# Joining the running maximum and the row sums of an attention sweep with VectorE instead of TensorE transposes

## The chip, the cores and the metric

The kernel runs on one core of a Trainium2 chip. The core has five engines that each take their instructions in a fixed order and wait for each other through semaphores: TensorE (PE, matrix products and transposes; its weight loads are listed apart as PEld), VectorE (DVE), ScalarE (ACT), GpSimd (POOL) and SyncE (SP, which here only issues DMAs). SBUF is the on-chip memory of 128 partitions, PSUM the memory that PE writes. Only PE, DVE and ACT touch PSUM.

The metric is the time of one execution on the device in microseconds (us); the median of the runs counts.

## The reference

One encoder layer over 2048 tokens of width 1024. One input projection feeds two mixers, a gated linear attention (group A) and a dense softmax attention with compressed keys and values (group B). Their outputs go side by side through one output projection, and a LayerNorm closes the layer. The change sits mainly in group B:

```python
def attend(blk):
    qn, qr = blk
    s = (jnp.einsum('bqhd,bkhd->bhqk', qn, k_nope) + jnp.einsum('bqhr,bkr->bhqk', qr, k_r))
    p = jax.nn.softmax(s, axis=-1)
    return jnp.einsum('bhqk,bkhv->bqhv', p.astype(v.dtype), v)
```

There are 4 heads and 2048 queries; the softmax runs over all 2048 keys. All arrays are float32.

## The kernel before

The program has four stages: sweep A (linear attention, first pass, to about 330 us), sweep C (second pass, and the projections that make queries and keys, to about 580 us), the attention, and the output projection with its LayerNorm, whose first part overlaps the end of the attention.

**The attention** works through 16 blocks, each one head times 512 queries (`QB`). Scores are kept transposed: keys on the 128 partitions, the 512 queries along the free axis. A block has 8 key pairs `j` of 2 x 128 keys. A float32 product is made of several fp32r products of high and low parts. Per block and pair:

- `scores` (L1599 to L1603): 10 matmuls into a PSUM tile `pS` of 128 x 2 x 512; two such tiles alternate.
- `copy` (ACT, L1608): the scores to an SBUF tile `s`.
- `smax` (DVE, L1618 and L1621): the running maximum over keys, `rm`, 128 x 512, from each half of `pS`.
- `sub` (DVE, L1645), `exp` (ACT, L1649), `phi` (ACT, high part `ph`, L364), `plo` (POOL, low part `pl`, L370), `pv` (6 matmuls into `o`, L418 to L420).
- `acc`: the sum of the exponentials, on DVE for pairs 0, 1, 2, 5 (PSUM tile `ap`, L1672), on POOL for pairs 3, 4, 6, 7 (SBUF tile `acc`, L1675 and L1677).

At the end of a block, the maximum must be joined over the 128 partitions and spread back: `tmax` (L1627) transposes `rm` on PE in 4 pieces into the PSUM tile `mx`; `rmax` (L1632) reduces it on DVE to `mc`, 128 x 4; `bmax` (L1639) transposes the broadcast `mc` on PE back into `mb`, one maximum per query on all partitions. `sub` needs `mb`. Likewise the sums: `tot` (L1695, L1696) adds the two partial sums into `acc`; `tsum` (L1708) transposes it on PE in 4 pieces into `sx`; `rcp` (L1714, L1715) reduces and inverts on DVE; `keep` (L1720) stores the 512 results to DRAM from ACT's queue.

**The order** is written out: every step has a place in units of one key pair (tables `PLACE`, `PLACE_LAST`), all steps are sorted by place, and each engine executes its instructions in just that order. While block `i` ends, PE already works on the scores of block `i+1` and on the `pv` products of block `i-1`. Sweep C is ordered in the same way by `PLACE_C`, `PLACE_C_FIRST` and `PLACE_C_LAST`.

**The close** (`finish`): per 128 tokens the LayerNorm, with `rsqrt_b` (L437 to L440) as four tiny DVE instructions on 128 x 1 columns, and scalings of 128 x 512 (L2023, L2026).

Of the kernel before, what the change touches and what calls it, by code (L numbers as in the profile page):

```python
# [9 lines left out]
F32 = mybir.dt.float32  # L10
# [3 lines left out]
ALU = mybir.AluOpType  # L14
AX = mybir.AxisListType
# [3 lines left out]
P = 128  # L19
# [10 lines left out]
QB = 512  # L30
# [43 lines left out]

SUM_DVE = (0, 1, 2, 5)
SUM_POOL = (3, 4, 6, 7)

# [65 lines left out]

PLACE_C = dict(
    skv=1.6,
    kvx=(1.12, 1.44),
    ipa=(-0.08, 0.695),
    ipb=(-0.014, 0.701),  # L150
    ipc=(0.026, 0.723),
# [3 lines left out]
    pqr=(0.849, 1.355),  # L155
    tq=(1.13, 1.56),
    xh=(-0.19, -0.054),
    sqO=(0.272, 0.988),
    rgl=(0.283, 1.029),
    sqm=(0.14, 0.858),  # L160
    rml=(0.352, 0.993),
# [13 lines left out]
    ssm=(0.277, 0.958),  # L175
    rmd=(0.401, 1.006),
# [47 lines left out]
    kvx=(1.18, 1.5),  # L224
# [9 lines left out]
    sqO=(0.469, 0.999),  # L234
    rgl=(0.603, 1.027),
    sqm=(0.073, 0.865),
    rml=(0.101, 0.976),
# [13 lines left out]
    ssm=(0.095, 0.913),  # L251
    rmd=(0.194, 1.009),
# [41 lines left out]
    sqO=(0.15, 0.435),  # L294
    rgl=(0.229, 0.457),
    sqm=(0.101, 0.657),
    rml=(0.162, 0.878),
    cq=(0.463, 1.041),
    ckv=(0.35, 1.075),
    vh=(0.865, 1.252),  # L300
# [7 lines left out]
    ss=(0.166, 0.454),  # L308
    rgd=(0.332, 0.461),
    og=(0.336, 0.508),  # L310
    ssm=(0.103, 0.733),
    rmd=(0.254, 1.022),
    krf=(0.139, 0.6),
    cqTl=(0.598, 1.211),
    ckvTl=(0.88, 1.703),
# [37 lines left out]
class K:  # L353
# [80 lines left out]

    def rsqrt_b(self, u, y, t, w, r):
        nc = self.nc
        nc.vector.tensor_tensor(t, y, u, ALU.mult)  # L437
        nc.vector.tensor_tensor(w, t, y, ALU.mult)
        nc.vector.tensor_scalar(t, w, -0.5, 1.5, ALU.mult, ALU.add)
        nc.vector.tensor_tensor(r, t, y, ALU.mult)  # L440
        return r
# [1133 lines left out]
    def attention(self):  # L1575
        tc, nc = self.tc, self.nc
        mm = nc.tensor.matmul
        V, G, Ac = nc.vector, nc.gpsimd, nc.scalar
        NP = NKT // 2
        with ExitStack() as ctx:  # L1580
# [29 lines left out]
            def smax(i, j):  # L1610

                d = stt[i]
                s = d["s"][j]
                ps = d["ps", j]
                src = s if i == 0 else ps
                if j == 0:
                    d["rm"] = self.keep.tile([P, QB], F32, tag="rm", name=f"rm{i}")
                    V.tensor_tensor(d["rm"], src[:, 0], s[:, 1], ALU.max)  # L1618
                else:
                    for e in range(2):  # L1620
                        V.tensor_tensor(d["rm"], src[:, e], d["rm"], ALU.max)  # L1621

            def tmax(i):
                d = stt[i]
                d["x"] = pX.tile([P, 4, P], F32, tag="x", name=f"mx{i}")
                for e in range(4):
                    nc.tensor.transpose(d["x"][:, e], d["rm"][:, e * P:(e + 1) * P], self.ident)  # L1627

            def rmax(i):
                d = stt[i]  # L1630
                d["mc"] = bs.tile([P, 4], F32, tag="mc", name=f"mc{i}")
                V.tensor_reduce(d["mc"], d["x"], AX.X, ALU.max)  # L1632

# [27 lines left out]
            def acc0(i):  # L1661
                d = stt[i]
                d["ap"] = pA.tile([P, QB], F32, tag="ap", name=f"ap{i}")
                Ac.activation(d["ap"], d["s"][SUM_DVE[0]][:, 0], AF.Copy)

            def acc(i, j):
                d = stt[i]
                s = d["s"][j]
                if j in SUM_DVE or i == nb - 1:
                    for e in range(2):  # L1670
                        if j != SUM_DVE[0] or e:
                            V.tensor_tensor(d["ap"], d["ap"], s[:, e], ALU.add)  # L1672
# [25 lines left out]
            def close(i, shape, name, other):  # L1698


                p, tag = other if i == nb - 1 else (pX, "x")
                return p.tile(shape, F32, tag=tag, name=name)

            def tsum(i):
                d = stt[i]
                d["x"] = close(i, [P, 4, P], f"sx{i}", (pA, "ap"))
                for e in range(4):
                    nc.tensor.transpose(d["x"][:, e], d["as"][:, 0, e * P:(e + 1) * P], self.ident)  # L1708

            def rcp(i):  # L1710

                d = stt[i]
                rc = bs.tile([P, 4], F32, tag="rc", name=f"rc{i}")
                V.tensor_reduce(rc, d["x"], AX.X, ALU.add)  # L1714
                V.reciprocal(rc, rc)  # L1715
                d["rc"] = rc

            def keep(i):
                h, b = blocks[i]
                Ac.dma_start(self.r_s[b][:, h].rearrange("o (e p) -> p (o e)", p=P), stt[i]["rc"])  # L1720

            def turn(i):

# [58 lines left out]
            own = (("tot", tot), ("tsum", tsum), ("rcp", rcp), ("keep", keep), ("oh", oh), ("ol", ol), ("y", y), ("yc", yc))  # L1782
            own_late = tuple(e for e in own if e[1] is not keep)
            for i in range(nb):
                for j in range(NP):
                    t = NP * i + j
                    put(t, scores, i, j)
                    for n, f in (("copy", copy), ("max", smax), ("sub", sub), ("exp", exp), ("hi", phi), ("lo", plo),
                                 ("pv", pv), ("acc", acc)):
                        if n != "acc" or j != SUM_POOL[0] or i == nb - 1:  # L1790
                            put(t + at(n, i, j), f, i, j)
                put(NP * i + at("acc0", i), acc0, i)
                for n, f in (("tmax", tmax), ("rmax", rmax), ("bmax", bmax)) + {nb - 1: (), nb - 2: own_late}.get(i, own):
                    put(NP * i + NP - 1 + at(n, i), f, i)
                if i + 2 < nb:
                    put(NP * i + 4.05, self.fetch, i + 2)

# [69 lines left out]
            for c in range(4, NCH):  # L1867
                with fixed():
                    split(c + 2)
                    load(c + 4)  # L1870
                    if 4 < c < NCH - 1:
                        op.load_res(rest[c + 1])
                    op.product(rest[c])
                    op.finish(rest[c])
                with self.after(*last.values()), fixed():
                    for f in {4: (tot, oh, ol), 5: (tsum, rcp), 7: (turn, y, rows, yc)}.get(c, ()):
                        f(nb - 1)
                    if c == 6:
                        turn(nb - 2)
                        rows(nb - 2)  # L1880
# [217 lines left out]
```

## Time and profile before

| | us |
|---|---|
| median of 3 runs (lowest, highest) | 1267.62 (1267.16, 1270.45) |
| the profiled execution | 1266.33 |
| its span, first to last instruction | 1264.5 |
| PE busy in the span | 1242.3 |
| DVE busy | 906.0 |
| ACT busy | 725.8 |
| POOL busy | 721.7 |

The span is 1.8 us shorter than the profiled execution's own time, and that execution is 1.3 us below the median. A timeline row of the profile reads: start (us), duration (us), engine, line, operation, output<-inputs, shape, xcount, and in brackets the idle time of the engine before it with what ended it. Rows that say x2 or more merge instructions that follow each other. A matmul's duration overlaps that of the next, so what a matmul costs is the distance from its start to the next start. On the other engines too the next instruction often starts some tens of ns before the row of the last has ended.

### The profile page before, as it was taken

Reading aid. Unit: us, or ns where it says so; the run is one execution under the profiler, and the core shown is the slowest. Engines: PE = TensorE matmul, PEld = TensorE weight load, DVE = VectorE, ACT = ScalarE, POOL = GpSimd, SP = SyncE. Lnnn points to the kernel's source line nnn. Section 1 sums busy time; section 2 is a strip of 40 time slices with the busy share of each in tenths; the row PEclk is TensorE's granted clock in tenths of the full one; section 3 lists DMA queues with packets and bytes.
Section 4 is the critical chain, followed back from the end, with each engine's and each line's share of the span. In section 5 each row is a group of like instructions: output and inputs, shape, how many; then the busy total and the mean of one; then the engine's idle time right before and its main releaser. Section 6 shows DMA issues by size and latency. Waiting matters only on the chain.

```text
span 1264.5 us, 19632 instructions
## 1 busy us (share of the span) xinstructions
PE 1242.3 (98%) x6890; PEld 1094.2 (87%) x6890; DVE 906.0 (72%) x1654; ACT 725.8 (57%) x1149; POOL 721.7 (57%) x443
## 2 busy tenths in 40 slices
PE   8999999999999999999999999999999999999997
PEld 7999999999899999988788888888888888887886
DVE  6635555554565666575988888888888888379998
ACT  7543443444664545445788888788888888411110
POOL 0132323223364555421798888889999999935441
PEclk9999999999999999999999999999999999999999
DMA  8224655556757788868422222202244120477773
GB/s 294 79 81 123 139 143 139 144 135 159 268 179 212 227 244 239 240 183 195 73 37 48 41 43 43 59 9 59 59 94 92 41 43 26 125 205 199 206 199 116
DMA packets 284338, 165.61 MB, mean 131 GB/s; under 512 B 185574, under 2 KB 241774, under 8 KB 284240
## 3 DMA queue, kind: packets, MB, share of 16 engines
q1 hardware_dynamic: 276176, 162.23, 48.2%
q0 software_dynamic: 672, 2.10, 0.4%
q8 instruction: 55, 0.90, 0.4%
q10 hardware_dynamic: 7392, 0.03, 0.3%
q14 instruction: 43, 0.35, 0.1%
HBM read 105.54 MB, written 58.75 MB: 130 GB/s over the span
## 4 chain that ended last, share of the span: by engine, by line
PE 86%; DVE 5%; DMA 3%; issue 2%; SPq 2%; ACT 1%; POOL 1%; DVEq 0%; POOLq 0%; ACTq 0%
PE pz L1266 7%; PE ipm L1335 5%; PE o L418 5%; PE o L419 5%; PE o L420 5%; PE pS L1599 4%; PE pS L1600 4%; PE pS L1602 4%; PE pS L1601 4%; PE pS L1603 4%; PE ipa L418 4%; PE ipa L420 4%; PE ipa L419 4%; PE ipg L420 2%; PE ipg L418 2%; PE ipg L419 2%
## 5 line engine op out<-in xcount | busy, mean ns | idle before, releaser
L370 POOL TENSOR_TENSOR pl<-s,ph 128x1024 fp32r<-128x1024 f32 x128 | 306.6, 2412 | 51.5 <-ACT ph L364 40.9
L1621 DVE TENSOR_TENSOR rm<-pS,rm 128x512 f32<-128x512 f32 x210 | 144.8, 690 | 36.3 <-ACT s L1608 30.7
L1608 ACT ACTIVATE s<-pS 128x1024 f32<-128x1024 f32 x128 | 131.3, 1025 | 60.4 <-PE pS L1603 50.0
L1645 DVE TENSOR_TENSOR s<-s,mb 128x1024 f32<-128x1024 f32 x128 | 151.2, 1213 | 8.9 <-PE mb L1639 8.8
L364 ACT ACTIVATE ph<-s 128x1024 fp32r<-128x1024 f32 x128 | 135.0, 1057 | 16.7 <-PE o L420 16.1
L1649 ACT ACTIVATE s<-s 128x1024 f32<-128x1024 f32 x128 | 131.4, 1049 | 9.4 <-DVE s L1645 9.3
L418 PE MATMUL ipa<-wah,xah 128*128 128x384 f32 (+1 forms) x384 | 128.8, 335 | 5.4 <-ACT wah L364 5.4
L419 PE MATMUL ipa<-wal,xah 128*128 128x384 f32 (+1 forms) x384 | 124.6, 324 | 0.0
L420 PE MATMUL ipa<-wah,xal 128*128 128x384 f32 (+1 forms) x384 | 124.4, 324 | 0.0
L1085 POOL TENSOR_TENSOR Sb<-Sb,Us 64x512 f32<-64x512 f32 x15 | 19.9, 1325 | 170.1 <-DVE Us L1077 161.0
L1599 PE MATMUL pS<-qh,kvT 128*128 128x512 f32 x256 | 102.4, 400 | 0.8 <-DVE rm L1621 0.4
L418 PE MATMUL o<-ph,vh 128*128 128x512 f32 x256 | 101.0, 395 | 0.0
L1600 PE MATMUL pS<-ql,kvT 128*128 128x512 f32 x256 | 99.9, 390 | 0.0
L1602 PE MATMUL pS<-rh,kvT 128*128 128x512 f32 x256 | 99.9, 390 | 0.0
L1601 PE MATMUL pS<-qh,kvT 128*128 128x512 f32 x256 | 99.8, 390 | 0.0
L1603 PE MATMUL pS<-rl,kvT 128*128 128x512 f32 x256 | 99.7, 390 | 0.0
L420 PE MATMUL o<-ph,vl 128*128 128x512 f32 x256 | 99.7, 389 | 0.0
L419 PE MATMUL o<-pl,vh 128*128 128x512 f32 x256 | 99.6, 389 | 0.0
L1672 DVE TENSOR_TENSOR ap<-ap,s 128x512 f32<-128x512 f32 x120 | 83.1, 693 | 2.7 <-ACT s L1649 0.8
L370 POOL TENSOR_TENSOR ol<-of,oh 128x512 fp32r<-128x512 f32 x32 | 43.7, 1365 | 67.8 <-ACT oh L364 62.5
L418 PEld LDWEIGHTS ipa<-wah,xah 128*128 128x128 f32 x384 | 73.1, 190 | 8.3 <-ACT wah L364 5.4
L419 PEld LDWEIGHTS ipa<-wal,xah 128*128 128x128 f32 x384 | 73.1, 190 | 1.0 <-DVE wal L370 0.5
(303 smaller groups left out, 3416.1 us busy)
## 6 DMA issues: line engine op xcount, KB each, us to landing
xcf<-xT_dram SPq DMA_DIRECT2D x16, 512.0 KB, 5.7
xr<-x_dram SPq DMA_DIRECT2D x16, 512.0 KB, 5.9
out_dram<-rr SPq DMA_DIRECT2D x32, 256.0 KB, 2.1
xaf<-xT_dram SPq DMA_DIRECT2D x14, 512.0 KB, 4.1
oib<-oi_s SPq DMA_DIRECT2D x16, 256.0 KB, 4.9
qdb<-qd_s SPq DMA_DIRECT2D x16, 256.0 KB, 3.7
SU<-su_s SPq DMA_DIRECT2D x16, 256.0 KB, 4.8
ub<-u_s SPq DMA_DIRECT2D x16, 256.0 KB, 4.5
```

The source lines that it names most:

```text
L364: return nc.scalar.activation(dst, src, AF.Copy).ins
L370: return e.tensor_tensor(dst, src, hi.bitcast(F32), ALU.subtract).ins
L418: mm(out, ah, bh, start=start, stop=False)
L419: mm(out, ah, bl, start=False, stop=False)
L420: mm(out, al, bh, start=False, stop=stop)
L1599: mm(ps[:, e], kh, qh, start=True, stop=False)
L1600: mm(ps[:, e], kh, ql, start=False, stop=False)
L1601: mm(ps[:, e], kl, qh, start=False, stop=False)
L1602: mm(ps[:, e], kr, rh, start=False, stop=False)
L1603: mm(ps[:, e], kr, rl, start=False, stop=True)
L1621: V.tensor_tensor(d["rm"], src[:, e], d["rm"], ALU.max)
L1645: V.tensor_tensor(s, s, d["mb"][:, None, :].to_broadcast([P, 2, QB]), ALU.subtract)
```

## The change

The edit has four parts.

1. **Maximum (blocks 1 to 10, `WIDE`).** `rm` becomes 128 x 2 x 512 in SBUF, a tile of the pool `xfp`. Pair 0 does nothing; pair 1 takes the maximum of its PSUM tile and pair 0's SBUF copy; pairs 2 to 7 take one 128 x 1024 instruction each instead of two of 128 x 512. The join no longer uses PE transposes: DVE takes the maximum of the two halves, transposes within 32 x 32 blocks, reduces to 128 x 16, folds the four 32-partition quadrants by two copies and one maximum, and writes the result to `mc` by four 32 x 4 instructions. `bmax` stays, at place 1.9 instead of 1.48.
2. **Sums (blocks 0 to 13).** A new step `tpart` does the same kind of transposing and reducing on DVE, to 128 x 16; `tsum` is then one PE transpose instead of four, `rcp` works on 16 x 32, and `keep` stores 16 rows of 32 values.
3. **`rsqrt_b` for one column** takes three `tensor_scalar` instructions with per-partition scalars instead of three `tensor_tensor` and one `tensor_scalar`. Only `finish` has one column.
4. **Places** in sweep C: `kvx` of each step's first chunk, `sqO` of each step's second, and `rml`, `ssm` of the last step.

```diff
+WIDE = range(1, 11)
-    tsum=12.04,
+    tpart=11.25,
+    tsum=12.44,
...
-    kvx=(1.12, 1.44),
+    kvx=(1.3, 1.44),
...
     def rsqrt_b(self, u, y, t, w, r):
         nc = self.nc
+        if u.shape[1] == 1:
+            nc.vector.tensor_scalar(t, y, u, y, ALU.mult, ALU.mult)
+            nc.vector.tensor_scalar(t, t, -0.5, 1.5, ALU.mult, ALU.add)
+            nc.vector.tensor_scalar(r, t, y, None, ALU.mult)
+            return r
...
+                if i in WIDE:
+                    if j == 1:
+                        d["rm"] = self.xfp.tile([P, 2, QB], F32, tag="xf", name=f"rm{i}")
+                    if j:
+                        V.tensor_tensor(d["rm"], ps, d["s"][0] if j == 1 else d["rm"], ALU.max)
+                    return
...
             def tmax(i):
                 d = stt[i]
+                if i in WIDE:
+                    rm = d["rm"]
+                    V.tensor_tensor(rm[:, 0], rm[:, 0], rm[:, 1], ALU.max)
+                    V.transpose(rm[:, 1], rm[:, 0])
+                    g = bs.tile([P, 2, QB // 32], F32, tag="m16", name=f"m16_{i}", bufs=1)
+                    V.tensor_reduce(g[:, 0], rm[:, 1].rearrange("p (b k) -> p b k", k=32), AX.X, ALU.max)
+                    V.tensor_copy(g[0:64, 1], g[64:128, 0])
+                    V.tensor_tensor(g[0:64, 0], g[0:64, 0], g[0:64, 1], ALU.max)
+                    V.tensor_copy(g[0:32, 1], g[32:64, 0])
+                    d["mc"] = bs.tile([P, 4], F32, tag="mc", name=f"mc{i}")
+                    for b in range(4):
+                        V.tensor_tensor(d["mc"][32 * b:32 * b + 32], g[0:32, 0, b::4], g[0:32, 1, b::4], ALU.max)
+                    return
...
+            def tpart(i):
+                d = stt[i]
+                V.transpose(d["as"][:, 1], d["as"][:, 0])
+                d["s16"] = bs.tile([P, QB // 32], F32, tag="s16", name=f"s16_{i}")
+                V.tensor_reduce(d["s16"], d["as"][:, 1].rearrange("p (b k) -> p b k", k=32), AX.X, ALU.add)
+
             def tsum(i):
                 d = stt[i]
+                if i < nb - 2:
+                    d["x"] = pX.tile([P, 4, P], F32, tag="x", name=f"sx{i}")[0:QB // 32, 0]
+                    nc.tensor.transpose(d["x"], d["s16"], self.ident)
+                    return
```

**Order of VectorE at the end of block 4, before** (the number behind a tile's name is its block, the second one the key pair; `ap3` is the sum of block 3, `s4` are scores of block 4):

```order
L1621 TENSOR_TENSOR rm4_8083<-pS4_6_8251,rm4_8083 128x512 x2
L1621 TENSOR_TENSOR rm4_8083<-pS4_7_8272,rm4_8083 128x512 x2
L1672 TENSOR_TENSOR ap3_8134<-ap3_8134,s3_5_7962 128x512 x2
L1632 TENSOR_REDUCE mc4_8335<-mx4_8324 128x4
L1618 TENSOR_TENSOR rm5_8361<-pS5_0_8307,s5_0_8346 128x512
L1645 TENSOR_TENSOR s4_2_8132<-s4_2_8132,mb4_8337 128x1024
```

**The same place after the change:**

```order
L1700 TENSOR_TENSOR ap3_8126<-ap3_8126,s3_5_7951 128x512 x2
L1640 TENSOR_TENSOR rm4_8110<-rm4_8110 128x512
L1641 STREAM_TRANSPOSE rm4_8110<-rm4_8110 128x512
L1643 TENSOR_REDUCE m16_4_8309<-rm4_8110 128x16
L1644 COPY m16_4_8309<-m16_4_8309 64x16
L1645 TENSOR_TENSOR m16_4_8309<-m16_4_8309 64x16
L1646 COPY m16_4_8309<-m16_4_8309 32x16
L1649 TENSOR_TENSOR mc4_8314<-m16_4_8309 32x4 x4
L1673 TENSOR_TENSOR s4_2_8124<-s4_2_8124,mb4_8333 128x1024
```

Where one reduction stood behind the two additions to `ap3`, ten instructions stand now, still behind those additions; six of the ten are `TENSOR_TENSOR` whose inputs both lie in SBUF (L1640, L1645, and L1649 four times).

**Order of TensorE from the last scores of block 5's pair 0 on, before** (`o3` is block 3's output):

```order
L1603 MATMUL pS5_0_8307<-rl5_7911,kvT_3892 128x512
L1627 MATMUL mx4_8324<-ident_213,rm4_8083 128x128 x4
L418 MATMUL o3_8200<-ph3_4_8242,vh_3893 128x512
L419 MATMUL o3_8200<-pl3_4_8305,vh_3893 128x512
L420 MATMUL o3_8200<-ph3_4_8242,vl_3894 128x512
L418 MATMUL o3_8200<-ph3_4_8242,vh_3893 128x512
L419 MATMUL o3_8200<-pl3_4_8305,vh_3893 128x512
L420 MATMUL o3_8200<-ph3_4_8242,vl_3894 128x512
L1639 MATMUL mb4_8337<-ident_213,mc4_8335 128x128 x4
L1599 MATMUL pS5_1_8350<-qh5_7902,kvT_3892 128x512
```

**After:**

```order
L1610 MATMUL pS5_0_8291<-rl5_7902,kvT_3892 128x512
L420 MATMUL o3_8187<-ph3_4_8228,vh_3893 128x512
L421 MATMUL o3_8187<-pl3_4_8289,vh_3893 128x512
L422 MATMUL o3_8187<-ph3_4_8228,vl_3894 128x512
L420 MATMUL o3_8187<-ph3_4_8228,vh_3893 128x512
L421 MATMUL o3_8187<-pl3_4_8289,vh_3893 128x512
L422 MATMUL o3_8187<-ph3_4_8228,vl_3894 128x512
L1667 MATMUL mb4_8333<-ident_213,mc4_8314 128x128 x4
L1606 MATMUL pS5_1_8338<-qh5_7893,kvT_3892 128x512
```

The four `mx` transposes are gone; the four `mb` transposes stand between the same matmuls as before, in spite of the new place number.

More of the change, by code (lines that the diff above doesn't have):

```diff
@@ L157 @@
     xh=(-0.19, -0.054),
-    sqO=(0.272, 0.988),
+    sqO=(0.272, 0.94),
     rgl=(0.283, 1.029),
@@ L310 @@
     og=(0.336, 0.508),
-    ssm=(0.103, 0.733),
-    rmd=(0.254, 1.022),
+    ssm=(0.1025, 0.733),
+    rmd=(0.29, 1.022),
     krf=(0.139, 0.6),
@@ L1712, in rcp @@
                 d = stt[i]
-                rc = bs.tile([P, 4], F32, tag="rc", name=f"rc{i}")
+                if i < nb - 2:
+                    rc = d["rc"] = bs.tile([QB // 32, 32], F32, tag="rc", name=f"rc{i}")
+                    V.tensor_reduce(rc, d["x"].rearrange("b (k q) -> b q k", k=4), AX.X, ALU.add)
+                    V.reciprocal(rc, rc)
+                    return
+                rc = bs.tile([P, 4], F32, tag="rc4", name=f"rc{i}")
                 V.tensor_reduce(rc, d["x"], AX.X, ALU.add)
@@ L1781, in attention @@
             put(9.9, self.lo, wv_l, wv, wv_h, "pool")
-            own = (("tot", tot), ("tsum", tsum), ("rcp", rcp), ("keep", keep), ("oh", oh), ("ol", ol), ("y", y), ("yc", yc))
-            own_late = tuple(e for e in own if e[1] is not keep)
+            own = (("tot", tot), ("tpart", tpart), ("tsum", tsum), ("rcp", rcp), ("keep", keep), ("oh", oh), ("ol", ol), ("y", y), ("yc", yc))
+            own_late = tuple(e for e in own if e[1] not in (keep, tpart))
             for i in range(nb):
@@ L1793, in attention @@
                 for n, f in (("tmax", tmax), ("rmax", rmax), ("bmax", bmax)) + {nb - 1: (), nb - 2: own_late}.get(i, own):
-                    put(NP * i + NP - 1 + at(n, i), f, i)
+                    put(NP * i + NP - 1 + (1.9 if n == "bmax" and i in WIDE else at(n, i)), f, i)
                 if i + 2 < nb:
```

6 lines of the change are left out of this document (4 added, 2 removed).

## The prediction

> **What bounds the kernel now.** I read the page's first part, then busy time by stretch, then the timelines of PE, DVE and POOL around one block's end.
>
> ```profile
> span 1264.5 us, 19632 instructions
> PE 1242.3 (98%) x6890; PEld 1094.2 (87%) x6890; DVE 906.0 (72%) x1654; ACT 725.8 (57%) x1149; POOL 721.7 (57%) x443
> ```
> ```profile
> 600.00:1060.00 460.00, 458.38 (x2104) 378.63 (x2103) 401.00 (x533) 384.42 (x413) 408.66 (x178) 1.00 0.26 51
> ```
>
> The second fence is the attention (columns: PE, PEld, DVE, ACT, POOL busy, granted clock, DMA share, GB/s). PE is never idle, so each PE instruction saved is time saved and each wait of PE is time lost. But DVE stands at 87% and POOL at 89%: whoever needs them at a given moment may find them taken.
>
> The end of block 2, on PE, DVE and POOL:
>
> ```profile
> 657.89 0.60 PE L1627 MATMUL mx<-ident,rm 128*128 128x128 f32 x4
> ...
> 658.56 0.39 PE L419 MATMUL o<-pl,vh 128*128 128x512 f32 x1
> 658.79 0.40 PE L420 MATMUL o<-ph,vl 128*128 128x512 f32 x1
> ...
> 659.70 0.60 PE L1639 MATMUL mb<-ident,mc 128*128 128x128 f32 x4
> ```
> ```profile
> 654.89 1.42 DVE L1621 TENSOR_TENSOR rm<-pS,rm 128x512 f32<-128x512 f32 x2 [0.85 <-ACT s L1608]
> 656.23 1.42 DVE L1672 TENSOR_TENSOR ap<-ap,s 128x512 f32<-128x512 f32 x2
> 658.52 0.69 DVE L1632 TENSOR_REDUCE mc<-mx 128x4 f32<-128x512 f32 x1 [0.87 <-PE mx L1627]
> ...
> 668.92 2.34 DVE L1645 TENSOR_TENSOR s<-s,mb 128x1024 f32<-128x1024 f32 x2
> 671.18 0.68 DVE L370 TENSOR_TENSOR ofl<-o,ofh 128x512 fp32r<-128x512 f32 x1
> ```
> ```profile
> 656.65 7.13 POOL L370 TENSOR_TENSOR pl<-s,ph 128x1024 fp32r<-128x1024 f32 x3
> ```
>
> The last maximum starts when ACT's copy releases it (654.89); the two additions to `ap`, as long as the two maxima ahead of them (656.23 - 654.89 = 1.34), are through at 657.57; `mc` ends at 659.21 (658.52 + 0.69); PE takes up `mb` at 659.70, in its turn and without waiting. From 656.65 to 663.78 POOL runs three `pl` of block 1 without a gap.
>
> **What saves.** The `mx` group: from its start to the second matmul behind it 0.67 us pass (658.56 - 657.89), of which one matmul is 0.23 (658.79 - 658.56): 0.44 us saved per block, 10 blocks. `sx` is four of the same transposes, now one.
>
> ```profile
> 14.92 0.27 PE L932 MATMUL lrT<-ident,lr 128*98 128x128 f32 x1
> 14.95 0.42 PE L420 MATMUL ipa<-wah,xal 128*128 128x384 f32 x1
> 15.21 0.33 PE L418 MATMUL ipa<-wah,xah 128*128 128x384 f32 x1
> 15.38 0.33 PE L419 MATMUL ipa<-wal,xah 128*128 128x384 f32 x1
> ```
>
> A lone transpose costs (15.21 - 14.92) - 0.17 = 0.12, so 0.44 - 0.12 = 0.32 us saved in 14 blocks.
>
> **What the new join costs.** First without hindrance. The 128x1024 maximum goes by `sub` (one input in SBUF, one in PSUM): (671.18 - 668.92) / 2 = 1.13 us, which is from 654.89 to 656.02; the two additions, which stay ahead of the join in DVE's order, 1.34, to 657.36. Then the chain, each step waiting for the last:
>
> ```profile
> L1529 DVE STREAM_TRANSPOSE oT<-og x16: 711/712/715, 367.8 to 562.6; 128x512 f32<-128x512 f32 x16
> ```
> ```profile
> 674.32 0.68 DVE L1714 TENSOR_REDUCE rc<-sx 128x4 f32<-128x512 f32 x1
> 675.03 0.18 DVE L1715 RECIPROCAL rc<-rc 128x4 f32<-128x4 f32 x1
> ```
> ```profile
> 406.97 0.17 DVE L438 TENSOR_TENSOR ipm<-rm_t,ipm 128x2 f32<-128x2 f32 x1
> 407.17 0.16 DVE L439 TENSOR_SCALAR rm_t<-ipm 128x2 f32<-128x2 f32 x1
> ```
>
> Joining the halves 0.73, transposing 0.75 (0.71 and the 0.03 between dependent rows), reducing 0.71, three small dependent steps at 0.20, four writes of `mc` about 0.37: 3.16 us, so `mc` at 660.52. Without `mx`, PE wants it at 659.70 - 0.44 = 659.26. Even undisturbed PE waits 1.3 us, more than the 0.76 saved.
>
> It won't be undisturbed. The close shows it:
>
> ```profile
> 1160.43 1.25 DVE L437 TENSOR_TENSOR ln_t<-ln_y,u 128x1 f32<-128x1 f32 x1
> 1161.71 1.21 DVE L438 TENSOR_TENSOR ln_t<-ln_t,ln_y 128x1 f32<-128x1 f32 x1
> 1162.96 0.15 DVE L439 TENSOR_SCALAR ln_t<-ln_t 128x1 f32<-128x1 f32 x1
> 1163.15 1.13 DVE L440 TENSOR_TENSOR ln_r<-ln_t,ln_y 128x1 f32<-128x1 f32 x1
> ```
> ```profile
> 1160.34 1.32 POOL L370 TENSOR_TENSOR ol<-of,oh 128x512 fp32r<-128x512 f32 x1 [4.52 <-ACT oh L364]
> 1161.63 2.64 POOL L1944 TENSOR_TENSOR of<-of,gr 128x512 f32<-128x512 f32 x2
> ```
> ```profile
> 1259.25 0.15 DVE L437 TENSOR_TENSOR ln_t<-ln_y,u 128x1 f32<-128x1 f32 x1
> ```
>
> L437 on 128x1 takes 0.15 us when POOL is quiet (1259.25) and 1.25 when POOL works, ending just as POOL's instruction ends (1161.66); L438 and L440 sit out the next two. L439, with one SBUF input, isn't held. So a DVE instruction with two SBUF inputs waits for the running POOL instruction, and POOL's next one starts right behind it. Today's maxima and additions have one input in PSUM. The new join has six with both in SBUF, exactly while POOL runs three `pl`.
>
> Worked through: the halves' maximum, ready at 657.36, waits for the first `pl` (to 659.03, a third of 7.13 on) and ends at 659.7; the second `pl` runs 659.7 to 662.1. Transpose, reduction and copy (single input) bring the 64x16 maximum to 661.35; it waits until 662.1, and the third `pl` runs 662.15 to 664.5. The second copy, then `mc` waits until 664.5. POOL's next `pl` needs `mb`, so the rest of `mc` is free: 664.9. PE waits 664.95 - 659.26 = 5.7 us.
>
> Bounds: if only the first of the six is held, 659.7 + 2.4 = 662.1, a wait of 2.85; if all small steps are held too, the same three `pl` still limit it, plus the steps left over, 0.45: 6.15. I take 5.7, from the row that shows three holds in a row.
>
> The Trainium skill (SBUF — State Buffer, Who interferes with whom) says that float32 copies within SBUF may also take both ports and contend with GpSimd. No row of this case has such a copy beside POOL work; by that rule the two copies are held too, which is the 6.15 and 4.5 us more in all.
>
> **The clock.** PE's longest waits in the whole span, behind that for the first weights, and the stretch in which the two `pqr` of them lie (near the end of sweep C):
>
> ```profile
> PE pqr L418 <- ACT cqT_h L364: 1.4, 1, 1.4
> PE pz L1266 <- DVE og L1523: 1.2, 2, 0.9
> PE pqr L420 <- DVE cqT_l L370: 1.2, 1, 1.2
> PE mb L1639 <- DVE mc L1632: 0.8, 1, 0.8
> PE pmb L420 <- POOL ol L370: 0.7, 1, 0.7
> ```
> ```profile
> 550.50:553.50 3.00, 0.67 (x3) 0.30 (x2) 2.86 (x14) 1.25 (x7) 0.95 (x3) 0.98 0.95 330
> 553.50:556.50 3.00, 2.83 (x9) 2.63 (x10) 2.83 (x12) 0.51 (x2) 2.56 (x2) 0.50 0.74 208
> ```
>
> PE was idle for 2.3 us of the first 3.0 (busy 0.67), and in the next 3.0 the granted clock is 0.50: some 1.5 us of matmul time lost. A wait of 5.7 us should do the same each time: between 0 and 2.9 (a slow stretch as long as the wait, at half speed); I take 1.6, a little above the row since the wait is longer.
>
> **The rest.** `tpart` adds 1.4 us of DVE (0.75 + 0.64) per block behind `tot`. The next place where DVE has slack is the maximum of pair 3:
>
> ```profile
> 672.39 1.42 DVE L1621 TENSOR_TENSOR rm<-pS,rm 128x512 f32<-128x512 f32 x2 [0.53 <-ACT s L1608]
> ```
>
> It takes up 0.53, and the two narrower maxima ahead of it give 0.4 back, so pair 3's maximum ends up to 0.5 us later. PE asks for its PSUM tile only two pairs on; I cost it at nothing, with up to 0.5 us per block if that cover is gone. DVE's net load per wide block: maxima 10.0 to 7.9, join +2.5, sums +1.3: from 87% to about 92% of an unstretched block, not a bound. POOL's order, SP's queue and `fetch` are unmoved; `keep`'s store, smaller in packets, stays behind the same ACT work. `rsqrt_b` frees DVE from three waits per chunk, but its two-input scalings (L2026) meet POOL instead, and of PE's waits above only that for `pmb` lies in the close, and it is for POOL; at the very end one dependent step goes, 0.2. In sweep C's last step `cqT_h` and `cqT_l` come earlier, ahead of `rm_l` and of the `kvx` transposes: of the 2.6 us waited for `pqr` I take half, 1.3, and 0.7 of the slow stretch: 2.0 (between 0 and 4.1, both whole). Elsewhere in C only the 1.2 for `pz` could go.
>
> **Sum.** Per wide block 5.7 + 1.6 - 0.44 - 0.32 = 6.5, ten blocks +65; four other blocks -1.3; C -2.0; end -0.2: +61.9. On the profiled execution, 1266.33 (span 1264.5 and 1.8 around it), 1328.2; with the 1.3 by which the median lies above it, 1329.5.
>
> **Rivals.**
> - *The port does not hold attention's joins; the bare chain decides.* For it: in the attention no DVE row is stretched today. Against it: none there has two SBUF inputs beside POOL work. Wait 1.3: 10 x (1.3 - 0.76) - 3.5 = +1.9, about 1270; with the clock falling each time, 1286. By the skill's rule (TensorE: Matmul & The Clock Gate, What's actually happening) the clock falls only after an idle window of some 3.4 us, so 1270; the rows above saw it fall after two waits of less than that. Chance 0.09, a third of it within the measurement.
> - *Only the first maximum is held.* Wait 2.85, clock 0 to 1.6: +17 to +33, 1285 to 1301. Chance 0.09.
> - *Faster: `mc` is ready when PE asks.* The place is `mb`'s entry in PE's order; the price is at most 10 x 0.44 + 14 x 0.32 + 2.2 = 11.1, 1256.5. It needs the wait below 0.76 us, so a chain of 2.6 us or less behind the additions instead of 3.16, and no hold. Chance 0.05.
>
> **Numbers.** The forecast has 0.75, the rivals 0.23, 0.02 a slower course (a longer slow stretch, more holds). The range reaches down into the second rival, 1292, and up to 6.15 + 2.9 - 0.76 = 8.3 per wide block, which makes 1347, and 0.5 per block for the lost cover in half of them, 1352; left out are the first and third rival and half of the second, 0.18, and the 0.02. Within 0.3% (3.8 us, what a measurement of this kernel can tell from no change) lies a third of the first rival, 0.03; faster 0.05; slower 0.92.
>
> **What would show it.** `L1640` some 2 us long and ending with a `pl`; `L1645` and the first `L1649` stretched likewise; PE idle before `mb` for DVE `mc` ten times, some 57 us; clock near 0.5 for 3 us behind each; no wait before `sx`. Wrong if the six rows last 0.7 and 0.16, or if POOL's three `pl` have moved.

## The result and the profile after

The changed kernel takes 1344.1 us (median of 5 runs, 1342.2 to 1346.1) against 1267.6: 1.060 times as long, 95% interval 1.0586 to 1.062. Predicted were 1329.5 and a range of 1292 to 1352.

The first part of the profile after, and the attention's window (columns PE, PEld, DVE, ACT, POOL busy, granted clock as a share of full speed, DMA share, GB/s):

```profile
span 1342.3 us, 19406 instructions
PE 1253.5 (93%) x6808; PEld 1098.5 (82%) x6808; DVE 958.9 (71%) x1676; ACT 727.3 (54%) x1149; POOL 729.3 (54%) x443
```
```profile
600.00:1060.00 460.00, 391.33 (x1656) 318.67 (x1656) 402.05 (x470) 316.94 (x338) 331.51 (x140) 0.92 0.22 45
```

PE, which was idle here for 1.6 us before, now is for 68.7 of 460 us, and its clock has fallen from 1.00 to 0.92. PE's waits over the whole span (us in all, times, longest) name one cause; the next in size, for the first weights, is 5.3 us:

```profile
PE mb L1667 <- DVE mc L1649: 68.2, 10, 8.1
```

Ten waits before `mb`, one per wide block (a block of `WIDE`). The starts of `mb` in blocks 2, 3 and 8, with the wait of each in brackets:

```profile
672.05 1.11 PE L1667 MATMUL mb<-ident,mc 128*128 128x128 f32 x4 [6.01 <-DVE mc L1649]
709.93 1.12 PE L1667 MATMUL mb<-ident,mc 128*128 128x128 f32 x4 [6.06 <-DVE mc L1649]
905.68 1.12 PE L1667 MATMUL mb<-ident,mc 128*128 128x128 f32 x4 [8.06 <-DVE mc L1649]
```

They are of two sizes: 6.0 to 6.1 in six blocks (2 to 7), 7.8 to 8.1 in four (1, 8, 9, 10). The end of block 3 on DVE and POOL shows how the first size comes about:

```profile
701.83 2.60 DVE L1640 TENSOR_TENSOR rm<-rm 128x512 f32<-128x512 f32 x1
704.47 0.71 DVE L1641 STREAM_TRANSPOSE rm<-rm 128x512 f32<-128x512 f32 x1
705.22 0.69 DVE L1643 TENSOR_REDUCE m<-rm 128x16 f32<-128x512 f32 x1
705.94 0.74 DVE L1644 COPY m<-m 64x16 f32<-64x16 f32 x1
706.72 2.26 DVE L1645 TENSOR_TENSOR m<-m 64x16 f32<-64x16 f32 x1
709.01 0.16 DVE L1646 COPY m<-m 32x16 f32<-32x16 f32 x1
709.21 0.66 DVE L1649 TENSOR_TENSOR mc<-m 32x4 f32<-32x4 f32 x4
```
```profile
701.48 7.47 POOL L372 TENSOR_TENSOR pl<-s,ph 128x1024 fp32r<-128x1024 f32 x3
```

Taken one by one, the three `pl` end at 703.89, 706.65 and 708.95. The halves' maximum lasts 2.60 us and ends 0.55 behind the first; a maximum of the same size with both inputs in SBUF takes 0.69 where POOL is idle (L1634, `rm<-s,rm`, in block 0). The first copy, 0.16 where nothing holds it (L1646 here), lasts 0.74 and ends behind the second `pl`; the 64x16 maximum, 2.26, ends with the third. The transpose and the reduction, with one input each, keep their 0.71 and 0.69. The holding goes both ways: the second `pl`, recorded from 703.83 while the halves' maximum still runs, lasts 2.82 us instead of 2.3 to 2.4.

In block 8 POOL has a fourth instruction behind the three `pl`, the low part of an output weight (`wol`), and it holds the first write of `mc`:

```profile
900.43 0.17 DVE L1645 TENSOR_TENSOR m<-m 64x16 f32<-64x16 f32 x1
900.63 2.20 DVE L1646 COPY m<-m 32x16 f32<-32x16 f32 x1
902.87 2.76 DVE L1649 TENSOR_TENSOR mc<-m 32x4 f32<-32x4 f32 x4
```
```profile
895.20 7.61 POOL L372 TENSOR_TENSOR pl<-s,ph 128x1024 fp32r<-128x1024 f32 x3
902.77 2.34 POOL L372 TENSOR_TENSOR wol<-wof,woh 128x1024 fp32r<-128x1024 f32 x1
```

The third piece is PE's pace behind the wait of block 3:

```profile
712.97 0.63 PE L1606 MATMUL pS<-qh,kvT 128*128 128x512 f32 x1
713.40 0.63 PE L1607 MATMUL pS<-ql,kvT 128*128 128x512 f32 x1
```
```profile
716.11 0.40 PE L420 MATMUL o<-ph,vh 128*128 128x512 f32 x1
716.34 0.39 PE L421 MATMUL o<-pl,vh 128*128 128x512 f32 x1
```

The matmuls start 0.43 us apart, and 0.23 from 715.9 on. Adding up what each start behind `mb` lies further than 0.2275 from the last, the slow stretches cost 1.3 to 2.9 us per block (they end 2.6 to 6.0 us behind `mb`'s start), 20.6 in all.

The 77.8 us between the two spans are thus: waits +68.2; slow stretches +20.6; the restart of PE's pipeline behind each wait, about 0.2 each (a matmul alone lasts 0.39 us where its start is 0.23 from the next), +2; `mx` -4.4; `sx` about -4.2; sweep C -1.8 (the first `mb` at 599.44, before 601.28); behind the last `mb` -1.6. That is 78.8, 1 us from the difference.

### The profile page after: what moved, and what is told of

It reads as the page before. It is cut to its first block, busy times and chain, and to the rows that moved or that the text cites. A ratio compares the mean times of both kernels' runs of the same rounds, so it can differ in the third digit from the quotient of the medians.

```text
span 1342.3 us, 19406 instructions
## 1 busy us (share of the span) xinstructions
PE 1253.5 (93%) x6808; PEld 1098.5 (82%) x6808; DVE 958.9 (71%) x1676; ACT 727.3 (54%) x1149; POOL 729.3 (54%) x443
## 4 chain that ended last, share of the span: by engine, by line
PE 79%; DVE 11%; DMA 3%; ACT 3%; issue 2%; SPq 2%; POOL 1%; DVEq 0%; ACTq 0%; POOLq 0%
PE pz L1273 5%; PE pS L1606 4%; PE pS L1607 4%; PE pS L1608 4%; PE pS L1609 4%; PE ipa L420 4%; PE pS L1610 4%; PE ipa L422 4%; PE ipa L421 4%; PE o L420 4%; PE o L421 4%; PE o L422 4%; PE ipm L1342 3%; PE po L422 2%; PE po L420 2%; PE po L421 2%
## 5 line engine op out<-in xcount | busy, mean ns | idle before, releaser
L372 POOL TENSOR_TENSOR pl<-s,ph 128x1024 fp32r<-128x1024 f32 x128 | 309.9, 2439 | 129.7 <-ACT ph L366 119.2
L1606 PE MATMUL pS<-qh,kvT 128*128 128x512 f32 x256 | 107.4, 419 | 0.5 <-DVE rm L1626 0.4
L1607 PE MATMUL pS<-ql,kvT 128*128 128x512 f32 x256 | 103.9, 406 | 0.0
L1608 PE MATMUL pS<-qh,kvT 128*128 128x512 f32 x256 | 103.7, 405 | 0.0
L1609 PE MATMUL pS<-rh,kvT 128*128 128x512 f32 x256 | 103.2, 403 | 0.0
L1610 PE MATMUL pS<-rl,kvT 128*128 128x512 f32 x256 | 102.6, 401 | 0.0
L1626 DVE TENSOR_TENSOR rm<-pS,rm 128x1024 f32<-128x1024 f32 x60 | 73.4, 1223 | 32.4 <-ACT s L1615 31.3
L1667 PE MATMUL mb<-ident,mc 128*128 128x128 f32 x64 | 14.8, 375 | 69.0 <-DVE mc L1649 68.2
```

What stands on the lines that cost most here:

```text
L372: return e.tensor_tensor(dst, src, hi.bitcast(F32), ALU.subtract).ins
L1606: mm(ps[:, e], kh, qh, start=True, stop=False)
L1607: mm(ps[:, e], kh, ql, start=False, stop=False)
L1608: mm(ps[:, e], kl, qh, start=False, stop=False)
L1609: mm(ps[:, e], kr, rh, start=False, stop=False)
L1610: mm(ps[:, e], kr, rl, start=False, stop=True)
```

## Experiments

All are edits of the changed kernel; times are medians, ratios are against the kernel before.

### No wide block

```diff
-WIDE = range(1, 11)
+WIDE = range(0)
```

> WIDE is empty: all 16 blocks take the narrow maxima and the PE transposes mx again; the joined sums, rsqrt_b and the places in sweep C stay changed. Theory (the wide blocks' join carries all of the loss): the PE waits before mb, 68.2 us in the changed kernel's trace, go, and with them the slow stretches behind them; what is left of the change is what the two traces show outside the wide blocks: 1.84 us earlier at the first mb (601.28 to 599.44), 0.32 per block from sx in 14 blocks (4.5), and some 1.6 in the close (between the last mb and the end). 1267.6 - 7.9 = about 1259.7, faster than before. Rival (the sums' new step tpart, 1.4 us of DVE per block, carries a part of the loss): a wait of PE for a DVE maximum or for sx appears in the blocks and the time is over 1264.

Measured: 1262.9 us, ratio 0.9959 (0.9944 to 0.9974): 0.4% less than before. Two neighbouring `mb`, which no wait precedes:

```profile
689.35 0.60 PE L1667 MATMUL mb<-ident,mc 128*128 128x128 f32 x4
720.15 0.60 PE L1667 MATMUL mb<-ident,mc 128*128 128x128 f32 x4
```

They are 30.80 apart (30.84 on average from block 1 to 13), before 31.12: 0.28 saved per block where 0.32 was forecast for `sx`, and `tpart` costs nothing here. The theory holds: the whole loss is the wide blocks'. The 3 us missed lie outside them: sweep C gave 0.9 in this profile, not 1.84, and the close lost 1.4 instead of winning 1.6. Between the profiles of all these kernels the first `mb` moves from 599.2 to 601.8, so the gain in sweep C is 0.8 on average and the single values are scatter.

### A join of single-input instructions

```diff
-                    V.tensor_tensor(rm[:, 0], rm[:, 0], rm[:, 1], ALU.max)
-                    V.transpose(rm[:, 1], rm[:, 0])
+                    half = pX.tile([P, 4, P], F32, tag="x", name=f"mx{i}").rearrange("p e q -> p (e q)")
+                    V.tensor_reduce(half, rm.rearrange("p a q -> p q a"), AX.X, ALU.max)
+                    V.transpose(rm[:, 1], half)
...
-                    V.tensor_copy(g[0:64, 1], g[64:128, 0])
-                    V.tensor_tensor(g[0:64, 0], g[0:64, 0], g[0:64, 1], ALU.max)
-                    V.tensor_copy(g[0:32, 1], g[32:64, 0])
+                    V.tensor_reduce(g[0:64, 1], g[64:128, 0, :, None], AX.X, ALU.max)
+                    V.tensor_reduce(g[0:64, 2], g[0:64, 0:2].rearrange("p a b -> p b a"), AX.X, ALU.max)
+                    V.tensor_reduce(g[0:32, 3], g[32:64, 2, :, None], AX.X, ALU.max)
...
-                        V.tensor_tensor(d["mc"][32 * b:32 * b + 32], g[0:32, 0, b::4], g[0:32, 1, b::4], ALU.max)
+                        V.tensor_reduce(d["mc"][32 * b:32 * b + 32], g[0:32, 2:4, b::4].rearrange("p a e -> p e a"), AX.X, ALU.max)
```

> The changed kernel with a join in which no instruction has two SBUF inputs and none is a copy: the halves' maximum becomes a reduction of 128x1024 into the PSUM tile mx, both copies, the 64x16 maximum and the four writes of mc become reductions over a short axis. Order and places stay. Theory (a shared port that POOL holds makes the join long): nothing in the join is stretched; its chain is an estimated 1.2 (1024 elements, as the 128x1024 maximum) + 0.75 + 0.71 + 0.6 + 0.4 = 3.65 us, a PE wait of 1.75 us before mb in place of 6.0 to 8.1. From 1259.7 (the rest of the change alone), less 4.4 for mx, plus 17.5: 1273 if the clock stays full, 1281 if each wait is followed by a slow stretch of its own length. Rival (the join is long on DVE by itself, or DVE is held by something other than its second SBUF input, as by any work of POOL): waits stay at 5 us or more, 1325 to 1345.

Measured: 1292.8 us, ratio 1.0196 (1.0177 to 1.0216). DVE and POOL at the end of a block:

```profile
728.13 1.26 DVE L1641 TENSOR_REDUCE mx<-rm 128x512 f32<-128x1024 f32 x1
729.42 0.72 DVE L1642 STREAM_TRANSPOSE rm<-mx 128x512 f32<-128x512 f32 x1
730.17 0.69 DVE L1644 TENSOR_REDUCE m<-rm 128x16 f32<-128x512 f32 x1
730.89 0.17 DVE L1645 TENSOR_REDUCE m<-m 64x16 f32<-64x16 f32 x1
...
731.50 0.67 DVE L1650 TENSOR_REDUCE mc<-m 32x4 f32<-32x8 f32 x4
```
```profile
727.76 7.05 POOL L372 TENSOR_TENSOR pl<-s,ph 128x1024 fp32r<-128x1024 f32 x3
```
```profile
PE mb L1668 <- DVE mc L1650: 21.5, 10, 2.7
```

Beside the same three `pl` nothing is stretched, and the waits fall from 68.2 to 21.5 us. So it is neither the length of the join nor POOL's work as such, but the second SBUF input and the copies. The time is above the range given: the base, the version without wide blocks, is 3 us higher than was reckoned, the waits are 21.5 us for 17.5, and the clock falls more than either number assumed. Behind nine of the ten waits, most of them only 2.05 us long, PE runs at half pace for about 3.4 us (14.5 us in all, where 1281 had room for 8). 1261.1 (the span without wide blocks) - 4.4 + 21.5 + 14.5 = 1292.7, and the span is 1292.3; the restarts, some 2 us, are left out of this sum.

### Only the halves' maximum held

The join's last steps as in the last version, L1640 and L1641 as in the changed kernel.

```diff
-                    V.tensor_copy(g[0:64, 1], g[64:128, 0])
-                    V.tensor_tensor(g[0:64, 0], g[0:64, 0], g[0:64, 1], ALU.max)
-                    V.tensor_copy(g[0:32, 1], g[32:64, 0])
+                    V.tensor_reduce(g[0:64, 1], g[64:128, 0, :, None], AX.X, ALU.max)
+                    V.tensor_reduce(g[0:64, 2], g[0:64, 0:2].rearrange("p a b -> p b a"), AX.X, ALU.max)
+                    V.tensor_reduce(g[0:32, 3], g[32:64, 2, :, None], AX.X, ALU.max)
...
```

> The changed kernel with only the steps behind the block reduction made single-input reductions; the halves' maximum (L1640) stays a TENSOR_TENSOR of two SBUF inputs. This is the prediction's second rival as a kernel. Theory: L1640 still ends with the first pl (2.56 us), everything behind it runs at its bare length (0.75 + 0.72 + 0.6 + 0.4 = 2.47): a PE wait of some 3.05 us, 30.5 in ten blocks; 1259.7 - 4.4 + 30.5 = 1286 if the clock stays full, up to 1301 if it falls for 3 us behind each wait. By the Trainium skill (TensorE: Matmul & The Clock Gate, What's actually happening) the clock needs an idle window of some 3.4 us to fall, so 1286. Rival (the small steps are held by any POOL work): waits of 5 us or more, 1325 to 1345.

Measured: 1302.9 us, ratio 1.028 (1.0262 to 1.0298); waits of 33.1 us, 3.35 in nine blocks. L1640 keeps its 2.56 us, the small steps their 0.16 to 0.18. Of the changed kernel's wait of 6.0, some 3.35 are thus the halves' maximum with the bare chain, and the other 2.65 the holds of the small steps. The clock, by two of the ten waits:

```profile
699.84 1.12 PE L1667 MATMUL mb<-ident,mc 128*128 128x128 f32 x4 [3.35 <-DVE mc L1649]
735.29 0.65 PE L1667 MATMUL mb<-ident,mc 128*128 128x128 f32 x4 [3.34 <-DVE mc L1649]
```

Waits of one length, and `mb` runs at half pace behind the one and at full pace behind the other. Four of the ten have no slow stretch, six have one, 12.7 us in all; neither "none" nor "always" was right. The time lies 2 us above the 1301 given for "always", as the waits are 2.6 us longer and the base 3 us higher than was reckoned.

### Only the copies held

The single-input join with both `tensor_copy` back in.

```diff
-                    V.tensor_reduce(g[0:64, 1], g[64:128, 0, :, None], AX.X, ALU.max)
+                    V.tensor_copy(g[0:64, 1], g[64:128, 0])
...
-                    V.tensor_reduce(g[0:32, 3], g[32:64, 2, :, None], AX.X, ALU.max)
+                    V.tensor_copy(g[0:32, 3], g[32:64, 2])
```

> As the version in which no join instruction has two SBUF inputs, but the second copy (32x16) stays a copy, and the first (64x16) too. Theory A (copies take the second port too, as the 64x16 copy of 0.74 us in place of 0.16 in the changed kernel suggests, and as the Trainium skill says in SBUF — State Buffer, Who interferes with whom): each copy waits for the pl then running: the first ends some 1.5 us late, the second with the third pl: a PE wait of about 5 us, 1325. Theory B (only two-input instructions are held; the 0.74 has another cause): a wait of 1.75 us as with no copies at all, 1273 to 1281.

Measured: 1321.2 us, ratio 1.0423 (1.0407 to 1.044); waits of 5.0 to 5.4 us in blocks 1 to 7 and 3.5 in blocks 8 to 10. Block 4, and then block 8, each with POOL:

```profile
740.52 1.61 DVE L1645 COPY m<-m 64x16 f32<-64x16 f32 x1
742.16 0.18 DVE L1646 TENSOR_REDUCE m<-m 64x16 f32<-64x32 f32 x1
742.37 2.04 DVE L1647 COPY m<-m 32x16 f32<-32x16 f32 x1
```
```profile
737.38 7.00 POOL L372 TENSOR_TENSOR pl<-s,ph 128x1024 fp32r<-128x1024 f32 x3
```
```profile
892.40 0.18 DVE L1646 TENSOR_REDUCE m<-m 64x16 f32<-64x32 f32 x1
892.61 0.16 DVE L1647 COPY m<-m 32x16 f32<-32x16 f32 x1
```
```profile
892.90 2.35 POOL L372 TENSOR_TENSOR pl<-s,ph 128x1024 fp32r<-128x1024 f32 x1 [0.57 <-ACT ph L366]
```

Beside POOL's work the copies last 1.61 and 2.04 us and end with a `pl`; in block 8 POOL happens to be idle from 892.33 to 892.90, and the same copy takes 0.16. Theory A holds: a float32 copy within SBUF waits for POOL like a two-input instruction.

### The output weight moved away

```diff
-    pre_lo=3.57,
+    pre_lo=4.5,
```

> The changed kernel with POOL's low part of the output weights (wol, in blocks 8, 9 and 10 right behind the three pl that run beside the join) moved behind the next block's first two pl. Theory (each POOL instruction that follows without a gap holds one join instruction more): the waits before mb in blocks 8, 9 and 10 fall from 8.06 to the 6.0 of the other blocks, 6.2 us in all, 1338. Rival (those blocks wait longer for another reason): they stay at 8.

Measured: 1343.1 us, ratio 1.0597 (1.058 to 1.0613), no different from the changed kernel. In block 8 the wait falls from 8.06 to 5.96 as expected. In blocks 9 and 10 it stays at 7.8, for a new reason: the later `wol` pushes POOL's next work back, so that the sum of pair 7 (`acc`, to 935.8 in block 9) now runs into the join and holds L1640 ahead of the three `pl`. That is what block 1 of the changed kernel shows too, where `acc` ends at 625.8 and L1640 at 626.35. So a fourth POOL instruction costs one more hold here, be it `wol` or `acc`; which joins meet four depends on how late POOL is.

### Keeping PE busy in the wait

```diff
                 d["mb"] = pM.tile([P, QB], F32, tag="mb", name=f"mb{i}")
+                for _ in range((33 if i in (1, 8, 9, 10) else 24) if i in WIDE else 0):
+                    mm(d["mb"], self.vh[:, 0], self.qt[i + 1][0], start=True, stop=True)
```

> The changed kernel, with matmuls of 128x512 into the mb tile ahead of the mb transposes, which overwrite what they leave: 24 in six of the wide blocks (5.5 us), 33 in blocks 1, 8, 9 and 10 (7.5 us). They use only operands that are there already, and keep PE busy while it waits for mc. Nothing else moves. It prices the clock: theory (the slow stretches, 20.6 us in all in the changed kernel's trace, come from PE's idleness alone): PE's pitch is full right behind mb, and the time falls by about 20, to 1323. Rival (PE is slow behind the wait for another reason, as the burst of ACT, DVE and POOL work that mb lets go): the time stays at 1344.

Measured: 1327.3 us, ratio 1.0473 (1.0458 to 1.0488), 16.8 less than the changed kernel. Block 3 again:

```profile
703.39 5.60 PE L1667 MATMUL mb<-qh,vh 128*128 128x512 f32 x24
709.69 0.65 PE L1669 MATMUL mb<-ident,mc 128*128 128x128 f32 x4 [0.70 <-DVE mc L1649]
...
710.41 0.40 PE L1607 MATMUL pS<-ql,kvT 128*128 128x512 f32 x1
710.65 0.40 PE L1608 MATMUL pS<-qh,kvT 128*128 128x512 f32 x1
```

`mc` is no earlier, yet the matmuls behind `mb` start 0.23 apart at once, and no slow stretch is left in any block. The slow pace comes from PE's own idleness. From the first `mb` to that of block 11 (1003.65) 401.9 us pass, in the changed kernel 421.0 (to 1020.48): 19 of the 77 us lost are its price. The rest of the expected 20 went where the first `mb` is at 601.74 in this profile, 2.3 later than in that of the changed kernel.

### `mb` later on PE

```diff
-                    put(NP * i + NP - 1 + (1.9 if n == "bmax" and i in WIDE else at(n, i)), f, i)
+                    put(NP * i + NP - 1 + (2.38 if n == "bmax" and i in WIDE else at(n, i)), f, i)
```

> The changed kernel with one number other: bmax of the wide blocks at 2.38 in place of 1.9, which puts the mb transposes behind the ten score matmuls of the next block's pair 1 and the six pv matmuls after them (16 x 0.2275 = 3.64 us of PE work that needs nothing of the join). The join and its holds stay. Theory (PE loses only because it comes to mb too early): the waits shrink from 6.0 to 2.4 in six blocks and from 8.05 to 4.4 in four, 32 us in all, the slow stretches to about 1.6 each: from the version without wide blocks 1262.9 - 4.4 + 32 + 16 = 1306. Rival (the join holds up DVE, and PE meets DVE's lateness elsewhere): the waits before mb shrink, but PE waits for a maximum (L1626) before scores instead, and the time stays over 1330.

Measured: 1318.5 us, ratio 1.0411 (1.0394 to 1.0428), between the two theories. The waits before `mb` fall to 27.3 us, a little less than expected. But PE now waits 10.9 us, in 13 places, for a maximum (L1626) before scores, and 2.8 for `ofl` before `pv`: both mechanisms are at work.

### The single-input join with `mb` later

```diff
-                    put(NP * i + NP - 1 + (1.9 if n == "bmax" and i in WIDE else at(n, i)), f, i)
+                    put(NP * i + NP - 1 + (2.05 if n == "bmax" and i in WIDE else at(n, i)), f, i)
```

> The version in which no join instruction has two SBUF inputs or is a copy, with bmax at 2.05: mb behind the ten score matmuls of the next block's pair 1, 2.28 us of PE work against the waits of 2.05 that this join left (2.34 and 2.74 in two blocks). Theory: no wait and no slow stretch is left, and the mx transposes are saved: 1262.9 - 4.4 = 1258.5, faster than before and than the version without wide blocks. Rival (with 29 us of work in a block of 30.4, DVE is full, and PE waits for a maximum before scores instead): 1263 or more.

Measured: 1275.6 us, ratio 1.0068 (1.0055 to 1.0081). The slow stretches are gone and the waits before `mb` too, but for 0.6 us in two blocks; yet the rival holds: PE waits for a maximum before scores, 8.1 us in ten places, and 2.9 for `ofl` before `pv`. DVE behind the `sub`s of a block, and the wait of PE that follows:

```profile
700.65 0.70 DVE L1735 STREAM_TRANSPOSE acc<-acc 128x512 f32<-128x512 f32 x1
701.39 0.69 DVE L1737 TENSOR_REDUCE s<-acc 128x16 f32<-128x512 f32 x1
701.99 1.21 DVE L1674 TENSOR_TENSOR s<-s,mb 128x1024 f32<-128x1024 f32 x1
703.12 1.22 DVE L1626 TENSOR_TENSOR rm<-pS,rm 128x1024 f32<-128x1024 f32 x1
```
```profile
704.39 0.50 PE L1606 MATMUL pS<-qh,kvT 128*128 128x512 f32 x1 [0.87 <-DVE rm L1626]
```

The two rows of `tpart` (700.65 to 702.08) stand ahead of the maximum that PE waits for, that of pair 2, whose PSUM tile the scores for pair 4 need.

### `tpart` later, and the pair-1 maximum first

```diff
-    tpart=11.25,
-    tsum=12.44,
-    rcp=13.55,
+    tpart=13.25,
+    tsum=13.6,
+    rcp=14.0,
```

> The version with a join of single-input instructions and mb at 2.05, and tpart moved in all 14 blocks from 11.25 to 13.25 (DVE: behind the next block's pair-3 maximum in place of ahead of its pair-2 maximum), tsum to 13.6, rcp to 14.0. Theory (in that version the 1.4 us of tpart no longer have cover: they stand between the subs and the pair-2 maximum that PE then waits for by 0.87): the wait before scores goes, 8.1 us by the rows and about 0.25 more per restart, 10.6 in all, and with the earlier ofl the 0.29 before pv too, up to 5.4: 1260 to 1265. Rival (the lateness comes from mb itself, and the pair-3 maximum is now late instead): 1273 or more, with the wait at another scores group.

and, in a second kernel, in addition

```diff
-                            put(t + at(n, i, j), f, i, j)
+                            put(t + (0.34 if n == "max" and j == 1 and i in WIDE else at(n, i, j)), f, i, j)
```

> As the version with tpart later, and in blocks 1 to 10 the maximum of pair 1 at 0.34 in place of 1.21, so that it stands ahead of the subs of the block before, in the 0.81 us in which DVE waits for mb there. Theory: another 0.8 us per block of room for DVE, so that no PE wait is left in the wide blocks: 1258.5, some 4 below the version without wide blocks (1262.9). Rival (nothing waited for DVE any more, or the sub, exp, ph chain is now late): the same as with tpart later, or up to 3 more.

Measured: 1284.9 and 1284.1 us, ratios 1.014 (1.0125 to 1.0155) and 1.0138 (1.012 to 1.0156): slower than without these edits. Neither theory came true. The first time lies in its rival's range, but not by its mechanism; the second is the first again, as its own rival said. The waits before the scores for pair 4 are gone, as meant, but in their place the first of the two kernels has

```profile
PE sx L1743 <- DVE s L1737: 10.0, 14, 1.0
...
PE mb L1668 <- DVE mc L1650: 5.1, 10, 0.5
```

The sums' transpose now stands ahead of `tpart`'s end in PE's order, and the join is late again by 0.5. The 1.4 us of `tpart` find no free place at either spot. The slots that I chose were not searched for, so this shows two bad places and not that there is no good one.

### The single-input join with the old sums

The version with `mb` at 2.05, and `tpart`, `tsum`, `rcp` and `keep` as before the change.

```diff
...
-            own = (("tot", tot), ("tpart", tpart), ("tsum", tsum), ...
+            own = (("tot", tot), ("tsum", tsum), ...
...
```

> The version with a join of single-input instructions and mb at 2.05, with the row sums as they were before the change (no tpart, four sx transposes, rcp on 128x4). It asks what kept that version at 1275.6 where 1258.5 was expected. Theory (the 1.4 us of tpart per block: with mb 2.3 us later on PE, DVE has no room left for them ahead of the pair-2 maximum): the PE wait of 0.87 before scores goes in every wide block, and the time is 1267.0 less 4.4 for mx and about 1 for sweep C: 1261 to 1264, although sx costs its 4.5 us again; up to 1267 if the 0.29 before pv stays. Rival (the late mb alone is enough, with or without tpart): the waits stay, and with sx's 4.5 us the time is 1275 to 1281.

Measured: 1262.9 us, ratio 0.9965 (0.9954 to 0.9976), 0.35% less than before. Two neighbouring `mb`:

```profile
690.88 0.60 PE L1667 MATMUL mb<-ident,mc 128*128 128x128 f32 x4
721.68 0.62 PE L1667 MATMUL mb<-ident,mc 128*128 128x128 f32 x4
```

They are 30.80 us apart (30.82 on average from block 2 to 10), and between 640 and 960 us PE waits for nothing. So it was the joined sums, and of their steps `tpart` alone adds to DVE's work: the wide maximum with a join that POOL can't hold saves 0.3 us per block, the joined sums save 0.3, and each works alone, but together they ask for more of DVE at one place than it has. This version and the one without wide blocks are equal at 1262.9, the fastest that was run.

## Why the prediction was right, and where its terms were off

**The bound.** Right: PE was full, and each wait before `mb` went straight into the time.

**Savings.** `sx` 0.28 measured for 0.32. For `mx` the version with the old sums saves 0.30 per wide block (31.12 to 30.82) for 0.44, with `mb` at another place.

**The bare chain.** Put at 3.16 us and a wait of 1.3. With a reduction of 1.26 in place of 0.73 for the halves, the measured wait is 2.05, so 1.5 for the prediction's form, an estimate from these rows since no run had that form unheld: right within 0.3. The first rival's wait of 1.3 was this one; its premise, that the port does not hold the joins, fell.

**The port.** Right in kind, and in size for L1640 (2.56 us; "some 2") and L1645 (2.26, in seven blocks). The step that failed is that the copy passes unheld: predicted 5.7 us with the copies free, 6.15 with them held, measured 6.0 to 6.1 in six blocks. So the three holds fall on L1640, the first copy and L1645, and not on L1640, L1645 and the first L1649; that last sign of the prediction (L1649 stretched) came only in blocks 8 to 10, where it took 2.25 us behind `wol`, and there L1645 passed in 0.17. The rule of the Trainium skill (SBUF — State Buffer, Who interferes with whom) that float32 copies may take both ports was the better of the two: alone, the copies lasted 1.61 and 2.04 us. The second rival's course, made a kernel of its own, had waits of 3.35, predicted 2.85.

**Three holds.** The sum, and its upper bound too, took it that "the same three `pl` still limit it". In four blocks a fourth POOL instruction, `wol` or `acc`, made it 7.8 to 8.1. This is the larger error: the mean wait is 6.8 for 5.7, 11 us in all, of which about 8 are these four blocks (four times 8.0 - 6.0). POOL's rows of one block had been taken for all ten. The profile before had the fourth instruction in block 8, right behind the last of the three `pl`:

```profile
849.01 2.42 POOL L370 TENSOR_TENSOR pl<-s,ph 128x1024 fp32r<-128x1024 f32 x1 [0.84 <-ACT ph L364]
851.39 2.41 POOL L370 TENSOR_TENSOR wol<-wof,woh 128x1024 fp32r<-128x1024 f32 x1
```

**The range.** That 1344.1 lies inside it is in part luck. Its upper end had no room for a fourth hold; what covered the 6.8 us was the room for the clock, 2.9 us per wait, of which 2.06 came. With 6.15 us and the 1.6 of the forecast the sum would have been 1334. The last step to 1352 is also mis-added: 0.5 us in half of the ten blocks is 2.5, so 1349.6, which is still above the measured time.

**The clock.** 1.6 us per wait predicted, 2.06 by the trace, and 19 us in all when taken away. The rule that it needs an idle window of some 3.4 us (the Trainium skill, TensorE: Matmul & The Clock Gate, What's actually happening) would have kept the clock in the single-input join; that kernel lost 14.5 us behind waits of 2 us. The row of the two `pqr` was the better guide.

**`tpart` at nothing.** Right in the changed kernel and without wide blocks. The cover was thin, though: with `mb` 2.3 us later it was gone, and its absence cost more than the 0.5 us per block set aside, 13 us in all (1275.6 to 1262.9, although `sx` is four transposes again there).

**The rest.** Sweep C gave 0.8 on average for 2.0; the end lies within scatter. The terms together: +61.9 predicted, +77.8 measured; 11 of the 16 missing are the waits, 5 the slow stretches.

## What to carry to other kernels

Before moving a reduction from PE to DVE, look at what POOL runs at that moment: where POOL runs without a gap, a chain of tiny SBUF instructions pays up to one whole POOL instruction for each with two inputs and each copy, so write its steps as reductions, or with an operand in PSUM. Read the neighbour's rows in every block, not in one. Where PE is full, a wait of two microseconds can cost nearly twice its length, and two changes that each fit into DVE's slack need not fit together.

## What was not expected of the hardware

**The clock follows a grid in time, not the length of the wait.** In the single-input join the nine slow stretches end at 667.9, 702.2, 736.4, 770.2, 804.5, 838.7, 872.6, 906.8 and 941.1 us: on average 34.14 us apart, ten times 3.414, while the blocks are 34.2 apart. `mb` drifts over this grid: its four transposes last 0.65 us up to 766.4, then 0.90, 0.95, 1.00, 1.06 and 1.11, the slow pace setting in a little earlier each time. The Trainium skill (TensorE: Matmul & The Clock Gate, What's actually happening) states a free-running window of 3.41 us, and the trace agrees; but it need not be wholly idle. On that grid (an estimate from these rows, carried back to block 1), an idle time of 2.05 us within one window lowered the clock, while block 1's wait of 2.74, of which some 1.9 fell into one window, did not; nor did four of the ten waits of 3 to 3.35 us in the version with only the halves' maximum held, which two windows can share. In the version of the changed kernel with `mb` later, five waits are of 1.86 or 1.87 us: on the grid of its own slow stretches the two that lie wholly in one window, in blocks 2 and 5, lowered the clock, and the three that two windows share did not. The threshold would then lie near 1.9 of 3.41 us in these blocks; no run set out to measure it.

**Between two POOL instructions, the one that starts first goes first.** In blocks 1 to 7 the 64x16 maximum is held behind the first copy; in blocks 8 to 10 it passes in 0.17 us and the next copy is held in its place. The starts tell the two apart. In block 3 the third `pl` starts at 706.61, ahead of the maximum at 706.72; in block 8 the maximum starts at 900.43 and the `pl` at 900.47, 0.1 us behind the second's end, since it waits for ACT's `ph`. It is so in all ten blocks, and in the thirty joins of the three other versions that keep this maximum and both copies, but for one in which the two start within 0.001 us of each other. No run set the order on purpose.
